# Tanh back to PSUM, factors and blocks on ScalarE, a scan laid out by place, 1.6 pieces of scan for a piece of projection

## The chip, the cores and the metric

One NeuronCore of a Trainium2 chip. The metric is the device time of one launch in microseconds (us), the median of several runs. All data are float32; where TensorE should work at more than one pass of reduced precision, operands are split into a high and a low part ("fp32r") and three products are added.

## The reference, cut to what matters

One layer of a hybrid backbone on 128 context tokens and 2048 latent tokens, 1024 wide:

```python
h = rmsnorm(x, norm_mix) * (1 + sc1) + sh1
u, z_s5, qkv, z_gdn, beta_raw, a_raw = split(dot(h, w_in))
s5_out  = s5_mixer(u, z_s5, ...)      # complex diagonal recurrence, both directions
gdn_out = gdn_mixer(qkv, z_gdn, ...)  # gated DeltaNet in chunks of 64, both directions
x = x + gt1 * dot(concat(s5_out, gdn_out), w_out)
h = rmsnorm(x, norm_mlp) * (1 + sc2) + sh2
x = x + gt2 * dot(square(relu(dot(h, w_mlp_in))), w_mlp_out)
```

Inside the S5 mixer each of 32 channel groups has 64 complex states per direction, `h[t] = abar * h[t-1] + bbar u[t]`, and the output is the real part of `C h` plus a skip, through gelu and a gate. Inside the DeltaNet mixer q, k and v pass a convolution of three taps and SiLU first; each chunk needs the inverse of a unit lower triangular matrix and a decay matrix `exp(g_i - g_j)`.

## The kernel before, in words

**Stages.** The program runs through four stages. Up to some 320 us: setup, the u projection (`first_pass`), the tables of the recurrence (`s5_setup`, `s5_tables`). From some 320 to 1100 us the projection stage: for each of four groups of 512 tokens (0, 3, 1, 2) `group_h` builds the normed rows and `group_proj` multiplies them with the columns of `w_in`, block by block; group 0 stands alone, with the modulation's weights streamed beside it. Then a short stage with the remaining gate columns (`ZCOLS`) and the sequential DeltaNet steps. From some 1412 us to the end phase C: output projection and MLP.

**Work beside the projection.** Generators give up control at each `yield`. After each piece of projection, `Side.go` adds a rate to an account and runs that many pieces of the side work: `first` (DeltaNet, per group: `gdn_front`, `gdn_back`), `second` (`gdn_p2`), `third` (`gdn_p3`) and `scans` (eight parts `s5_part`, 15 pieces each). The rate of `scans` is 2 in the projection stage (L1734) and 3 in the next (where `second.rate, third.rate, scans.rate` are set). The program is then ordered on each engine by a planner's own timeline, so a rate sets an order of birth, and the planner what comes out of it.

**Eviction, `evac` L479.** A block of a projection (258 or 387 columns in a PSUM bank of the pool `psd`, three banks) goes through five operations: ScalarE takes the middle tap (L491), VectorE adds the two others from the bank (L493, L495), ScalarE takes tanh (L497) into a tile `ec2` of SBUF, VectorE forms (tanh + 1) * y (L499), and a DMA writes the result to DRAM. The bank's last reader is L495.

**Factors.** In `gdn_back` the decay matrix E of a chunk and direction (128 x 4 heads x 128) comes from four exponentials (L696) and is multiplied by a factor per row and head on GpSimd (L697); VectorE uses it at once. In `gdn_load` the loaded keys are multiplied by their decay in the same way (L873). In `gdn_p3`, which joins the inverses of blocks of 32 to a block of 128, the rows `RW` of four blocks come by DMA and GpSimd spreads them over block diagonal tiles TA and R by multiplying them, repeated, with a mask Mh or Mb of zeros and ones (L762, L764).

**The scan, `s5_part` L1254.** One part handles four channel groups, in both directions; a lane holds 8 sequences (2 directions, real and imaginary, 2 groups) of 272 elements in time order, one sequence behind the other, each with 17 super-chunks of 16 places. One element here stands for 8 tokens, whose inner steps are in the tables. First, for places 1 to 15, all super-chunks at once take one step of the recurrence (L1301 two products, L1303 and L1305 sums): every operand is read or written every 16th element. Then 15 steps carry the state from one super-chunk to the next, one after the other (L1323, L1325, L1326, on 16 and 8 elements). Then the entering states, times the powers of abar, are added to all elements (GpSimd product L1335, VectorE sum L1338). TensorE reads the states for the output (L1356), for the backward direction in reverse order.

**What the page calls them.** Tile names are those in the code: E, KVr, R, TA, Hin, S, T (for `T1`), gs (a PSUM bank of the scan), d (a bank of the projection), ec (the eviction's tiles).

Of the kernel before, what the change touches and what calls it, by code (L numbers as in the profile page):

```python
# [478 lines left out]
def evac(k, ct, ps, n, segs, off):  # L479
    nc = k.nc  # L480
    S = k.S
    if ct < 8:
        z = k.pe.tile([128, k.pew], F32, name="ec1")
        nc.scalar.activation(z[:, 0:n], ps[:, off:off + n], AF.Tanh, scale=0.5)
        nc.vector.tensor_scalar(z[:, 0:n], z[:, 0:n], 0.25, 0.25, op0=OP.mult, op1=OP.add)
        for (o, m, tk) in segs:
            nc.sync.dma_start(S['tz'][(ct - 4) * 128:(ct - 3) * 128, tk:tk + m], z[:, o:o + m])
    elif ct < 20:
        q = ct - 8
        t1 = k.pe.tile([128, k.pew], F32, name="ec1")  # L490
# [8 lines left out]
        nc.vector.scalar_tensor_tensor(o_[:, 0:n], th[:, 0:n], 1.0, y2[:, 0:n], op0=OP.add, op1=OP.mult)  # L499
# [51 lines left out]
def gdn_setup(k):  # L551

    nc = k.nc
    k.Mb = k.ga.tile([128, 4], F32, name="Mb")
# [14 lines left out]
    nc.gpsimd.memset(k.Mb, 0.0)  # L569
    nc.gpsimd.memset(k.Mh, 0.0)  # L570
    for b in range(4):
        nc.gpsimd.memset(k.Mb[32 * b:32 * b + 32, b:b + 1], 1.0)
        nc.gpsimd.memset(k.Mh[32 * b:32 * b + 32, b % 2:b % 2 + 1], 1.0)
# [175 lines left out]
def gdn_p3(k, cs):  # L749
# [6 lines left out]
    TA = k.ga.tile([128, 2, 4, 64], F32, name="TA")[:, 0:n]  # L756
    R = [k.ga.tile([128, 2, 4, 128], F32, name=f"R{d}")[:, 0:n] for d in range(2)]
    for j, c in enumerate(cs):
        nc.sync.dma_start(RW[:, j].rearrange("p d w h c->p (d w h) c"), dap(S['rw'], c * 65536, [[32, 128], [4096, 16], [1, 32]]))
        for d in range(2):  # L760
            pairs, a, e = PAIRS[d]
            nc.gpsimd.tensor_tensor(TA[a, j].rearrange("p h (b c)->p h b c", b=2), RW[a, j, d, 1, :, None, :].to_broadcast([64, 4, 2, 32]),  # L762
                                    k.Mh[a, None, :, None].to_broadcast([64, 4, 2, 32]), op=OP.mult)
            nc.gpsimd.tensor_tensor(R[d][:, j].rearrange("p h (b c)->p h b c", b=4), RW[:, j, d, 0, :, None, :].to_broadcast([128, 4, 4, 32]),  # L764
                                    k.Mb[:, None, :, None].to_broadcast([128, 4, 4, 32]), op=OP.mult)
# [279 lines left out]
def s5_setup(k):  # L1045
# [81 lines left out]
    for t_, e in ((k.tab8, 1), (k.tabL, 16)):  # L1127
        nc.vector.tensor_copy(t_[:, 0, 0], P8[:, 0, :, e])
        nc.vector.tensor_copy(t_[:, 0, 1], P8[:, 0, :, e])
        nc.vector.tensor_copy(t_[:, 1, 0], P8[:, 1, :, e])  # L1130
        nc.vector.tensor_scalar(t_[:, 1, 1], P8[:, 1, :, e], -1.0, None, op0=OP.mult)
# [122 lines left out]
def s5_part(k, hb):  # L1254
# [36 lines left out]
    def cols(t):  # L1291

        return t.rearrange("p r (d c)->p d r c", d=2)[:, :, :, c0:c0 + 2]
    TB8 = sb.tile([128, 2, 8], F32, name="tb8", bufs=1)
    TBL = sb.tile([128, 2, 8], F32, name="tbL", bufs=1)
    for t_, s_ in ((TB8, k.tab8), (TBL, k.tabL)):
        for j in range(2):
            V.tensor_copy(t_[:, j].rearrange("p (d r g)->p d r g", d=2, r=2), cols(s_[:, j]))
    for kk in range(1, 16):
        Tt = sb.tile([128, 2, 136], F32, name="Tt", bufs=1)  # L1300
        V.tensor_tensor(Tt.rearrange("p j (a s)->p j a s", a=8), sview(S, kk, [[0, 2], [272, 8], [16, 17]]), TB8[:, :, :, None].to_broadcast([128, 2, 8, 17]), op=OP.mult)  # L1301
        av = sview(S, 1 + kk, [[16, 136]])
        V.tensor_tensor(av, av, Tt[:, 0], op=OP.add)  # L1303
        sv = sview(S, 1 + kk, [[1088, 2], [544, 2], [16, 34]])
        V.tensor_tensor(sv, sv, Tt[:, 1].rearrange("p (d r a)->p d r a", d=2, r=2)[:, :, ::-1], op=OP.add)  # L1305
        if kk % 4 == 3:
            yield None
    for d in range(2):
        V.tensor_copy(k.NS[:, :, 16 * d + c0:16 * d + c0 + 2], sview(S, row(d, 0, 0) + 272 - 256 * d, [[544, 2], [272, 2]]))

    Hin = sb.tile([128, 2, 2, 2, 17], F32, name="Hin", bufs=1)
    H0 = Hin.rearrange("p d r g s->p (d r g s)")
    V.memset(sview(H0, 16, [[52, 2], [17, 4]]), 0.0)

    def hat(s_):
        return sview(H0, s_, [[69, 2], [17, 4]])

    def hat3(s_):
        return sview(H0, s_, [[69, 2], [34, 2], [17, 2]])
    V.tensor_copy(hat3(0), cols(k.h0))  # L1320
    for sc in range(15):
        Tb = sb.tile([128, 2, 8], F32, name="Tb", bufs=1)
        V.tensor_tensor(Tb.rearrange("p j (d a)->p j d a", d=2), sview(H0, sc, [[0, 2], [69, 2], [17, 4]]),  # L1323
                        TBL.rearrange("p j (d a)->p j d a", d=2), op=OP.mult)
        V.tensor_tensor(hat(sc + 1), sview(S, 1 + sc * 16 + 15, [[1088 + 16, 2], [272, 4]]), Tb[:, 0].rearrange("p (d a)->p d a", d=2), op=OP.add)  # L1325
        V.tensor_tensor(hat3(sc + 1), hat3(sc + 1), Tb[:, 1].rearrange("p (d r g)->p d r g", d=2, r=2)[:, :, ::-1], op=OP.add)  # L1326
    yield None
    for d in range(2):
        cs = slice(16 * d + c0, 16 * d + c0 + 2)
        for ri in range(2):  # L1330
            for j in range(2):
                oi = ri if j == 0 else 1 - ri
                tab = k.P8[:, j, cs, 1:17]
                T1 = sb.tile([128, 2, 17, 16], F32, name="T1", bufs=2)
                nc.gpsimd.tensor_tensor(T1, Hin[:, d, ri, :, :, None].to_broadcast([128, 2, 17, 16]),  # L1335
                                        tab[:, :, None, :].to_broadcast([128, 2, 17, 16]), op=OP.mult)
                sv = sview(S, row(d, oi, 0) + 1, [[1, 544]])
                V.tensor_tensor(sv, sv, T1.rearrange("p g s k->p (g s k)"), op=OP.subtract if ri == 1 and j == 1 else OP.add)  # L1338
        yield None

    for d in range(2):
        lat, ctx = (0, 256) if d == 0 else (16, 0)
        V.tensor_copy(sview(S, row(d, 0, 0) + lat, [[544, 2], [272, 2]]), k.h0[:, :, 16 * d + c0:16 * d + c0 + 2])
        V.memset(sview(S, row(d, 0, 0) + ctx, [[272, 4]]), 0.0)
# [527 lines left out]
```

## Time and profile before

| | |
|---|---|
| time, median of 3 runs | 3263.98 us (3262.58 to 3274.36) |
| profiled execution | 3273.32 us, its span 3271.5 us |
| mean granted TensorE clock | 0.949 of full speed |
| PE busy | 2968.4 us, 91% |
| VectorE (DVE) busy | 2012.6 us, 62% |
| GpSimd (POOL) busy | 1387.3 us, 42% |
| ScalarE (ACT) busy | 1106.4 us, 34% |
| DMA | 604.36 MB, 185 GB/s in the mean |

How to read it: busy time is the time in which an engine executes; PE stands for TensorE's matmuls. A page cuts the span in 40 slices of 82 us and gives each engine's busy share in tenths, so a stage is seen by its slices. A row of a view by lines gives busy time in us, mean ns of one, and the idle time before it with what ended it; rows of waits give us in total, times, and the longest. The rows on which the argument rests stand in a section of their own below.

### The profile page before, as it was taken

What the parts mean: (1) busy time and instruction counts of PE and PEld (TensorE: products, weight loads), DVE (VectorE), ACT (ScalarE), POOL (GpSimd) and SP (SyncE); (2) the same over time, 40 slices, a digit from 0 to 9 for tenths busy, and PEclk for the clock granted to TensorE, in tenths of its full rate; (3) what the DMA queues carried; (4) which work ended last, traced back from release to release, by engine and by line L of the source; (5) the groups of instructions that cost most, each with busy time, mean ns of one, the idle gap of its engine ahead of it and who ended that gap; (6) DMA issues with size and microseconds to landing.
All of it is one profiled execution on the core that took longest, in us unless ns stands there. A gap on an engine that the chain in (4) does not pass through costs nothing. (4 is left out here: it accounts for less than half of the span.)

```text
span 3271.5 us, 48561 instructions
## 1 busy us (share of the span) xinstructions
PE 2968.4 (91%) x17658; PEld 2520.8 (77%) x17658; DVE 2012.6 (62%) x3901; ACT 1106.4 (34%) x2325; POOL 1387.3 (42%) x1027
## 2 busy tenths in 40 slices
PE   5785879998898899988999999999999999999998
PEld 3673668787777777977887778898888887888886
DVE  5975587896877676346544367543458643684445
ACT  3442224543443221234333233322243322433332
POOL 3562232423345233146443454333444544554542
PEclk8887899999987999989999999999999999999999
DMA  9899967867667987989433455322434534553332
GB/s 261 198 182 258 332 207 229 262 216 240 206 204 237 285 279 255 361 289 328 138 103 107 147 166 166 100 78 78 139 123 150 150 94 126 164 170 98 99 95 71
DMA packets 573504, 604.36 MB, mean 185 GB/s; under 512 B 163020, under 2 KB 422208, under 8 KB 573264
## 3 DMA queue, kind: packets, MB, share of 16 engines
q1 hardware_dynamic: 573264, 601.25, 59.9%
q8 instruction: 139, 2.28, 0.3%
q14 instruction: 101, 0.83, 0.1%
HBM read 458.99 MB, written 142.14 MB: 184 GB/s over the span
## 5 line engine op out<-in xcount | busy, mean ns | idle before, releaser
L1400 POOL TENSOR_TENSOR wol<-woraw,woh 128x512 fp32r<-128x512 f32 x320 | 427.7, 1348 | 644.4 <-ACT woh L1399 629.1
L1550 DVE TENSOR_TENSOR acc<-acc,gA 128x512 f32<-128x512 f32 x510 | 340.9, 682 | 196.1 <-PE gA L1545 195.9
L1399 ACT ACTIVATE woh<-woraw 128x512 fp32r<-128x512 f32 x320 | 193.0, 626 | 777.3 <-PE gA L1545 467.9
L1545 PE MATMUL gA<-woh,ffH 128*128 128x512 f32 x1088 | 425.2, 391 | 5.7 <-ACT r L1527 3.2
L1545 PE MATMUL gA<-woh,ffL 128*128 128x512 f32 x1088 | 424.7, 390 | 1.9 <-DVE ffL L1531 1.9
L1545 PE MATMUL gA<-wol,ffH 128*128 128x512 f32 x1088 | 424.1, 390 | 0.0
L1400 POOL TENSOR_TENSOR wil<-wiraw,wih 128x1024 fp32r<-128x1024 f32 x128 | 327.2, 2557 | 114.3 <-PE gA L1523 81.9
L1530 DVE TENSOR_TENSOR r<-r 128x512 f32<-128x512 f32 (+1 forms) x160 | 167.1, 1051 | 306.5 <-ACT ffH L1529 306.2
L1523 PE MATMUL gA<-htH,wih 128*128 128x512 f32 (+1 forms) x1280 | 277.7, 362 | 4.5 <-DVE acc L1550 3.2
L1523 PE MATMUL gA<-htL,wih 128*128 128x512 f32 (+1 forms) x1280 | 272.8, 358 | 0.0
L1523 PE MATMUL gA<-htH,wil 128*128 128x512 f32 (+1 forms) x1280 | 271.8, 357 | 0.0
L471 PE MATMUL d<-hH,wh 128*128 128x258 f32 (+3 forms) x1152 | 212.7, 326 | 52.4 <-DMA wh<-s_wc 15.3
L1523 PEld LDWEIGHTS gA<-htH,wih 128*128 128x128 f32 x1280 | 223.3, 190 | 37.5 <-DVE acc L1550 4.5
L1523 PEld LDWEIGHTS gA<-htL,wih 128*128 128x128 f32 x1280 | 221.7, 188 | 30.8
L1523 PEld LDWEIGHTS gA<-htH,wil 128*128 128x128 f32 x1280 | 220.5, 188 | 29.9
L1545 PEld LDWEIGHTS gA<-woh,ffH 128*128 128x128 f32 x1088 | 204.8, 188 | 49.8 <-ACT r L1527 4.2
L1545 PEld LDWEIGHTS gA<-woh,ffL 128*128 128x128 f32 x1088 | 204.8, 188 | 44.1 <-DVE ffL L1531 2.3
L1545 PEld LDWEIGHTS gA<-wol,ffH 128*128 128x128 f32 x1088 | 204.8, 188 | 42.8
L471 PEld LDWEIGHTS d<-hH,wh 128*128 128x128 f32 x1152 | 178.7, 205 | 75.3 <-issue 31.9
L471 PE MATMUL d<-hL,wh 128*128 128x258 f32 (+3 forms) x1152 | 211.9, 319 | 3.6 <-DMA hL<-s_hL 3.5
L471 PE MATMUL d<-hH,wl 128*128 128x258 f32 (+3 forms) x1152 | 210.7, 321 | 3.3 <-DMA wl<-s_wc 3.3
L471 PEld LDWEIGHTS d<-hH,wl 128*128 128x128 f32 x1152 | 179.5, 202 | 17.3 <-issue 10.7
(387 smaller groups left out, 5407.4 us busy)
## 6 DMA issues: line engine op xcount, KB each, us to landing
wiraw<-in_w_mlp_in SPq DMA_DIRECT2D x128, 512.0 KB
woraw<-in_w_mlp_out SPq DMA_DIRECT2D x256, 256.0 KB
wl<-s_wc SPq DMA_DIRECT2D x68, 512.0 KB
wh<-s_wc SPq DMA_DIRECT2D x68, 512.0 KB
wada<-in_w_ada SPq DMA_DIRECT2D x48, 512.0 KB
KVr<-s_kv SPq DMA_DIRECT2D x34, 512.0 KB
Qr<-s_qkv SPq DMA_DIRECT2D x32, 512.0 KB
woraw<-in_w_out SPq DMA_DIRECT2D x64, 256.0 KB
```

The costliest lines, as they stand in the source:

```text
L471: nc.tensor.matmul(ps[:, 0:w], W_[:, kk, :], X_[kk][:, f:f + w], start=(n == 0), stop=(n == 23))
L1399: nc.scalar.activation(h[:, i:i + n], w, AF.Copy)
L1400: sub.tensor_tensor(l[:, i:i + n], w, h[:, i:i + n].bitcast(F32), op=OP.subtract)
L1523: nc.tensor.matmul(ps[b][:, 0:w], W[:, kk, :], X[:, kk, b * w:b * w + w], start=(m == 0), stop=(m == 23))
L1530: nc.vector.tensor_tensor(r[:, 0:w], r[:, 0:w], r[:, 0:w], op=OP.mult)
L1545: nc.tensor.matmul(ps, X[:, s], W[:, hf], start=(m == 0), stop=(m == 3 * FB - 1))
L1550: nc.vector.tensor_tensor(accs[i][:, c], accs[i][:, c], ps, op=OP.add)
```

## The change

Five edits are made together.

- `evac`: tanh (L497) writes to the block's own PSUM bank, and L499 reads it there.
- `gdn_back` and `gdn_load`: the GpSimd products L697 and L873 become four ScalarE operations each (copy with a scale per row), one for each head.
- `gdn_p3`: TA and R are persistent tiles, zeroed once in `gdn_setup`; ScalarE copies the blocks that are not zero, 12 copies for each call in place of two GpSimd products for each of the two directions and each chunk of the call.
- `s5_part`, `s5_setup`, `lane_tables`: the states are laid out by place: element 17 * place + super-chunk, with the row stride 289, so that one place of all super-chunks lies side by side. The carry over the super-chunks goes in four doubling steps over all of them, with a table `tabs` of five powers (1, 16, 32, 64, 128) in place of 15 single steps. ScalarE writes the input (L1287) and TensorE reads the states (L1356) with a stride of 17.
- the rate of the scans in the projection stage goes from 2 to 1.6.

```diff
@@ evac
-        th = k.pe.tile([128, k.pew], F32, name="ec2")
-        nc.scalar.activation(th[:, 0:n], y2[:, 0:n], AF.Tanh)
+        th = ps[:, 0:n]
+        nc.scalar.activation(th, y2[:, 0:n], AF.Tanh)
...
@@ gdn_setup
+    k.TA = k.ga.tile([128, 2, 4, 64], F32, name="TA")
+    k.R = [k.ga.tile([128, 2, 4, 128], F32, name=f"R{d}") for d in range(2)]
+    for t in (k.TA, *k.R):
+        nc.gpsimd.memset(t, 0.0)
...
@@ gdn_back
-        nc.gpsimd.tensor_tensor(E, E, bc4(bb[:, d]), op=OP.mult)
+        for h in range(4):
+            nc.scalar.activation(E[:, h], E[:, h], AF.Copy, scale=bb[:, d, h:h + 1])
@@ gdn_p3
-        for d in range(2):
-            pairs, a, e = PAIRS[d]
-            nc.gpsimd.tensor_tensor(TA[a, j]..., RW[a, j, d, 1, :, None, :]..., k.Mh..., op=OP.mult)
-            nc.gpsimd.tensor_tensor(R[d][:, j]..., RW[:, j, d, 0, :, None, :]..., k.Mb..., op=OP.mult)
...
+    for d in range(2):
+        pairs, a, e = PAIRS[d]
+        for blk in range(4):
+            nc.scalar.activation(R[d][sl(blk), :, :, sl(blk)], RW[sl(blk), :, d, 0], AF.Copy)
+            if sl(blk).start in (a.start, a.start + 32):
+                nc.scalar.activation(TA[sl(blk), :, :, sl(blk % 2)], RW[sl(blk), :, d, 1], AF.Copy)
@@ gdn_load
-    nc.gpsimd.tensor_tensor(KV[:, 0], KV[:, 0], bc4(k.kd[:, c, d]), op=OP.mult)
+    for h in range(4):
+        nc.scalar.activation(KV[:, 0, h], KV[:, 0, h], AF.Copy, scale=k.kd[:, c, d, h:h + 1])
@@ s5_setup
-    for t_, e in ((k.tab8, 1), (k.tabL, 16)):
...
+    Ls = p.tile([128, 2, 4, 32], F32, name="Ls")
+    nc.vector.tensor_copy(Ls[:, :, 0], P8[:, :, :, 16])
+    for i in range(3):
+        cmul(nc.vector, Ls[:, 0, i + 1], Ls[:, 1, i + 1], Ls[:, 0, i], Ls[:, 1, i], Ls[:, 0, i], Ls[:, 1, i], tmp[:, :, 0])
+    for e in range(5):
...
@@ s5_part
-    S = su.tile([128, 1 + 8 * 272], F32, name="S")
+    E = su.tile([128, 8 * 289], F32, name="S")
...
-                nc.scalar.activation(o if d == 0 else o[:, ::-1], ps[:, 0:272], AF.Copy)
+                o = sview(E, r + 17, [[1, 17], [17, 16]]) if d == 0 else sview(E, r + 288, [[-1, 17], [-17, 16]])
+                nc.scalar.activation(o, ps[:, 0:272].rearrange("p (s c)->p s c", c=16), AF.Copy)
...
     for kk in range(1, 16):
-        V.tensor_tensor(Tt..., sview(S, kk, [[0, 2], [272, 8], [16, 17]]), TB8..., op=OP.mult)
-        av = sview(S, 1 + kk, [[16, 136]])
+        V.tensor_tensor(Tt..., sview(E, 17 * kk, [[0, 2], [289, 8], [1, 17]]), tab(0, 17), op=OP.mult)
+        av = sview(E, 17 * kk + 17, [[289, 8], [1, 17]])
...
-    for sc in range(15):
...
+    for i in range(4):
+        sh = 1 << i
+        n = 16 - sh
+        Tb = sb.tile([128, 2, 136], F32, name="Tt", bufs=1)[:, :, 0:8 * n].rearrange("p j (a s)->p j a s", a=8)
+        V.tensor_tensor(Tb, sview(Hin, 1, [[0, 2], [18, 8], [1, n]]), tab(1 + i, n), op=OP.mult)
+        hv = sview(Hin, 1 + sh, [[18, 8], [1, n]])
+        V.tensor_tensor(hv, hv, Tb[:, 0], op=OP.add)
+        hv = sview(Hin, 1 + sh, [[72, 2], [18, 4], [1, n]])
+        V.tensor_tensor(hv, hv, Tb[:, 1].rearrange("p (r a) s->p r a s", r=2)[:, ::-1], op=OP.add)
...
-                h = S[la, r:r + 272]
-                nc.tensor.matmul(y, CA[la, ri, d, g, :], h if d == 0 else h[:, ::-1],
+                h = sview(E[la], r, [[1, 17], [17, 16]]) if d == 0 else sview(E[la], r + 271, [[-1, 17], [-17, 16]])
+                nc.tensor.matmul(y, CA[la, ri, d, g, :], h,
@@ program
-            scans = Side(2, [s5_part(k, hb) for hb in range(8)])
+            scans = Side(1.6, [s5_part(k, hb) for hb in range(8)])
```

## Rows read from the trace of the kernel before

**Rows 1.** Slices of the page: busy tenths in 40 slices of the span.
```profile
PE   5785879998898899988999999999999999999998
DVE  5975587896877676346544367543458643684445
```
**Rows 2.** Stretches: from:to, length, PE, PEld, DVE, ACT, POOL, clock, DMA share, GB/s.
```profile
1600.00:3271.50 1671.50, 1627.69 (x7744) 1380.93 (x7743) 905.81 (x1168) 533.09 (x884) 767.71 (x472) 0.99 0.39 121
...
500.00:550.00 50.00, 48.12 (x363) 41.86 (x362) 36.02 (x94) 23.19 (x71) 8.18 (x7) 1.00 0.72 234
1050.00:1100.00 50.00, 47.92 (x402) 36.58 (x402) 26.05 (x51) 20.98 (x60) 19.53 (x20) 0.87 0.90 269
...
550.00:600.00 50.00, 44.76 (x322) 41.52 (x321) 49.83 (x165) 24.49 (x79) 17.72 (x14) 0.93 0.69 224
1100.00:1150.00 50.00, 39.19 (x315) 37.05 (x314) 41.71 (x124) 9.50 (x21) 9.56 (x9) 0.86 0.93 301
...
320.00:480.00 160.00, 126.19 (x673) 93.50 (x674) 116.22 (x277) 35.75 (x68) 45.19 (x28) 0.89 0.82 272
100.00:200.00 100.00, 81.34 (x675) 74.86 (x675) 93.16 (x193) 46.66 (x92) 70.73 (x49) 0.90 0.88 207
```
**Rows 3.** Waits of PE, 480 to 1150: us in total, times, longest us.
```profile
PE gT L691 <- DVE qn L650: 9.5, 6, 2.4
...
PE gT L649 <- ACT kv L639: 3.8, 4, 1.8
...
PE d L471 <- DVE Hin L1326: 0.3, 1, 0.3
```
**Rows 4.** First group: ACT's waits, and DVE and PE in time (start, us).
```profile
ACT ec L491 <- DVE ec L499: 34.3, 6, 9.0
...
369.39 0.62 DVE L495 SCALAR_TENSOR_TENSOR ec<-d,cw,ec 128x385 f32<-128x385 f32 x1
...
388.24 0.89 DVE L499 SCALAR_TENSOR_TENSOR ec<-ec,ec 128x385 f32<-128x385 f32 x2
...
417.95 2.06 PE L471 MATMUL d<-hH,wh 128*128 128x258 f32 x8 [7.52 <-DVE ec L495]
```
**Rows 5.** Scan by line (ns min/median/max) and by form (busy us, mean ns).
```profile
L1301 DVE TENSOR_TENSOR Tt<-S,tb x120: 586/621/1628, 308.3 to 1237.7; 128x272 f32<-128x272 f32 x120
L1305 DVE TENSOR_TENSOR S<-S,Tt x120: 367/395/2484, 310.1 to 1238.7; 128x136 f32<-128x136 f32 x120
L1325 DVE TENSOR_TENSOR Hin<-S,Tb x120: 153/168/2359, 333.8 to 1254.6; 128x8 f32<-128x8 f32 x120
...
L1323 DVE TENSOR_TENSOR Tb<-Hin,tbL 128x16 f32<-128x16 f32 x120 | 32.9, 274 | 1.3
L1325 DVE TENSOR_TENSOR Hin<-S,Tb 128x8 f32<-128x8 f32 x120 | 27.8, 232 | 1.4
...
L736 DVE TENSOR_TENSOR UB<-W,U 128x256 f32<-128x256 f32 x5 | 2.1, 421 | 0.0
```
**Rows 6.** GpSimd lines by form: busy us, mean ns, idle before and what ended it.
```profile
L697 POOL TENSOR_TENSOR E<-E,bb 128x512 f32<-128x512 f32 x34 | 40.8, 1199 | 119.9 <-ACT E L696 39.6 <-issue 20.0 <-DVE UB L736 9.4
L873 POOL TENSOR_TENSOR KVr<-KVr,kd 128x512 f32<-128x512 f32 x34 | 38.7, 1138 | 72.3 <-DMA KVr<-s_kv 65.2 <-PE gs L1356 7.0
...
L762 POOL TENSOR_TENSOR TA<-RW,Mh 64x256 f32<-64x256 f32 x34 | 24.2, 711 | 36.5 <-DMA RW<-s_rw 31.9 <-ACT UC L706 3.1
```
**Rows 7.** ScalarE lines of the sizes that the change adds, by form.
```profile
L973 ACT ACTIVATE o<-o,ors 128x128 f32<-128x128 f32 x68 | 21.9, 391 | 26.3 <-POOL ors L80 26.3
L703 ACT ACTIVATE UC<-Us 64x256 f32<-64x256 f32 x34 | 14.1, 415 | 54.5 <-DVE Us L700 51.6 <-PE g L801 2.4
```
**Rows 8.** The scan's output matmul, and ScalarE reads strided and contiguous, by form.
```profile
L1356 PE MATMUL gs<-S,CA 64*128 64x272 f32 x256 | 58.6, 445 | 19.0 <-DVE S L1344 19.0
...
L1271 ACT ACTIVATE WT<-T 128x512 f32<-128x512 f32 x8 | 8.6, 1070 | 6.5 <-PE gs L1351 6.5
L1216 ACT ACTIVATE WI<-gs 128x512 f32<-128x512 f32 x16 | 8.9, 584 | 7.2 <-DMA s_stab<-WI 3.7 <-PE gs L1215 3.4
```

More of the change, by code (lines that the diff above doesn't have):

```diff
@@ L495, in evac @@
         nc.vector.scalar_tensor_tensor(y2[:, 0:n], ps[:, 2:2 + n], k.cw[:, 2, q:q + 1], y[:, 0:n], op0=OP.mult, op1=OP.add)
[L496 to L497 removed]
+        th = ps[:, 0:n]
+        nc.scalar.activation(th, y2[:, 0:n], AF.Tanh)
         o_ = k.pe.tile([128, k.pew], F32, name="ec3")
[L499 removed]
+        nc.vector.scalar_tensor_tensor(o_[:, 0:n], th, 1.0, y2[:, 0:n], op0=OP.add, op1=OP.mult)
         for (o, m, tk) in segs:
@@ L553, in gdn_setup @@
     nc = k.nc
-    k.Mb = k.ga.tile([128, 4], F32, name="Mb")
-    k.Mh = k.ga.tile([128, 2], F32, name="Mh")
+    k.TA = k.ga.tile([128, 2, 4, 64], F32, name="TA")
+    k.R = [k.ga.tile([128, 2, 4, 128], F32, name=f"R{d}") for d in range(2)]
+    for t in (k.TA, *k.R):
+        nc.gpsimd.memset(t, 0.0)
     k.mr_neg = k.ga.tile([128, 2, 128], FR, name="mneg")
@@ L568, in gdn_setup @@
     nc.vector.tensor_copy(k.rsel, sel)
[L569 to L573, printed above, removed]
 def gdn_scalars(k, b):
@@ L755, in gdn_p3 @@
     RW = k.gx.tile([128, 2, 2, 2, 4, 32], F32, name="RW")[:, 0:n]
-    TA = k.ga.tile([128, 2, 4, 64], F32, name="TA")[:, 0:n]
-    R = [k.ga.tile([128, 2, 4, 128], F32, name=f"R{d}")[:, 0:n] for d in range(2)]
+    TA = k.TA[:, 0:n]
+    R = [r[:, 0:n] for r in k.R]
     for j, c in enumerate(cs):
         nc.sync.dma_start(RW[:, j].rearrange("p d w h c->p (d w h) c"), dap(S['rw'], c * 65536, [[32, 128], [4096, 16], [1, 32]]))
-        for d in range(2):
-            pairs, a, e = PAIRS[d]
[L762 to L765, printed above, removed]
     def sl(blk):
         return slice(32 * blk, 32 * blk + 32)
+    for d in range(2):
[4 more added lines that the diff above has]
+                nc.scalar.activation(TA[sl(blk), :, :, sl(blk % 2)], RW[sl(blk), :, d, 1], AF.Copy)
     pg = k.psI.tile([128, 512], F32, name="g3")
@@ L981 @@
 PI = float(np.pi)
-SCRATCH_S = {'ys': [512, 8, 272], 'stab': [4, 128, 5120], 'sp': [128, 1408]}
+SCRATCH_S = {'ys': [512, 8, 272], 'stab': [4, 128, 5120], 'sp': [128, 1792]}
 def exp_acc(k, out, x, tag):
@@ L1032, in lane_tables @@
     k.P8 = SP[:, 0:1088].rearrange("p (r c e)->p r c e", r=2, c=32)
-    k.tab8 = SP[:, 1088:1216].rearrange("p (j r c)->p j r c", j=2, r=2)
-    k.tabL = SP[:, 1216:1344].rearrange("p (j r c)->p j r c", j=2, r=2)
-    k.h0 = SP[:, 1344:1408].rearrange("p (r c)->p r c", r=2)
+    k.tabs = SP[:, 1088:1728].rearrange("p (e b j q)->p e b j q", e=5, b=8, j=2)
+    k.h0 = SP[:, 1728:1792].rearrange("p (r c)->p r c", r=2)
 def s5_load(k):
-    SP = k.sp.tile([128, 1408], F32, name="SPl")
+    SP = k.sp.tile([128, 1792], F32, name="SPl")
     k.nc.sync.dma_start(SP, k.S['sp'])
@@ L1065, in s5_setup @@
     lre, lim, ldt = lanes[:, 0], lanes[:, 1], lanes[:, 2]
-    SP = p.tile([128, 1408], F32, name="SP")
+    SP = p.tile([128, 1792], F32, name="SP")
     lane_tables(k, SP)
@@ L1125, in s5_setup, with to @@
     nc.vector.tensor_scalar(k.nPi, Pw[:, 1], -1.0, None, op0=OP.mult)
-    for t_, e in ((k.tab8, 1), (k.tabL, 16)):
[L1128 to L1131, printed above, removed]
+    Ls = p.tile([128, 2, 4, 32], F32, name="Ls")
[3 more added lines that the diff above has]
+    for e in range(5):
+        re_, im_ = [(P8[:, r, :, 1] if e == 0 else Ls[:, r, e - 1]).rearrange("p (d b g)->p b d g", d=2, b=8) for r in range(2)]
+        def to(j, r):
+            return k.tabs[:, e, :, j].rearrange("p b (r d g)->p b r d g", r=2, d=2)[:, :, r]
+        nc.vector.tensor_copy(to(0, 0), re_)
+        nc.vector.tensor_copy(to(0, 1), re_)
+        nc.vector.tensor_copy(to(1, 0), im_)
+        nc.vector.tensor_scalar(to(1, 1), im_, -1.0, None, op0=OP.mult)
     nc.sync.dma_start(k.S['sp'], SP)
@@ L1267, in s5_part @@
     nc.sync.dma_start(CA.rearrange("p r d g c->p (r d) (g c)"), dap(k.S['stab'], base + 2048 + hf * 256, [[5120, 128], [512, 4], [1, 256]]))
-    WE = sb.tile([128, 2, 17, 16], F32, name="T1", bufs=2).rearrange("p a b c->p (a b c)")[:, 0:512].rearrange("p (g e c)->p g e c", g=4, e=8)
+    WE = sb.tile([128, 2, 16, 17], F32, name="T1", bufs=2).rearrange("p a b c->p (a b c)")[:, 0:512].rearrange("p (g e c)->p g e c", g=4, e=8)
     nc.sync.dma_start(WE.rearrange("p g e c->p (g e c)"), dap(k.S['stab'], base + 4096 + hf * 512, [[5120, 128], [1, 512]]))
@@ L1271, in s5_part @@
     nc.scalar.activation(WT, WE.rearrange("p g e c->p g c e"), AF.Copy)
-    S = su.tile([128, 1 + 8 * 272], F32, name="S")
+    E = su.tile([128, 8 * 289], F32, name="S")
     def row(d, ri, g):
-        return (d * 4 + ri * 2 + g) * 272
+        return (ri * 4 + d * 2 + g) * 289
     for g in range(2):
@@ L1291, in cols, with tab @@
     def cols(t):
[L1293 to L1298, printed above, removed]
+        return t.rearrange("p r (d c)->p r d c", d=2)[:, :, :, c0:c0 + 2]
+    def tab(e, n):
+        return k.tabs[:, e, hb, :, :, None].to_broadcast([128, 2, 8, n])
@@ L1306, in s5_part @@
+        av = sview(E, 17 * kk + 17, [[289, 8], [1, 17]])
+        V.tensor_tensor(av, av, Tt[:, 0].rearrange("p (a s)->p a s", a=8), op=OP.add)
+        sv = sview(E, 17 * kk + 17, [[1156, 2], [289, 4], [1, 17]])
+        V.tensor_tensor(sv, sv, Tt[:, 1].rearrange("p (r a s)->p r a s", r=2, a=4)[:, ::-1], op=OP.add)
         if kk % 4 == 3:
             yield None
+    Hin = sb.tile([128, 144], F32, name="Hin", bufs=1)
+    V.memset(Hin, 0.0)
+    V.tensor_copy(sview(Hin, 1, [[72, 2], [36, 2], [18, 2]]), cols(k.h0))
@@ L1308, in s5_part @@
     for d in range(2):
[L1309 to L1320, printed above, removed]
@@ L1321, in s5_part @@
-    for sc in range(15):
[L1322 to L1326, printed above, removed]
+        V.tensor_copy(sview(Hin, 36 * d + 2, [[72, 2], [18, 2], [1, 15]]), sview(E, row(d, 0, 0) + 272 + d, [[1156, 2], [289, 2], [1, 15]]))
@@ new lines, in s5_part @@
+        V.tensor_copy(k.NS[:, :, 16 * d + c0:16 * d + c0 + 2], sview(E, row(d, 0, 0) + 272 + 16 - 16 * d, [[1156, 2], [289, 2]]))
+    for i in range(4):
[7 more added lines that the diff above has]
+        V.tensor_tensor(hv, hv, Tb[:, 1].rearrange("p (r a) s->p r a s", r=2)[:, ::-1], op=OP.add)
@@ L1327, in s5_part, with enter @@
     yield None
+    def enter(d, ri):
+        return (ri * 4 + d * 2) * 18 + 1 - d
     for d in range(2):
@@ L1332, in s5_part @@
                 oi = ri if j == 0 else 1 - ri
[L1333 to L1338, printed above, removed]
+                t = k.P8[:, j, cs, 1:17]
+                T1 = sb.tile([128, 2, 16, 17], F32, name="T1", bufs=2)
+                nc.gpsimd.tensor_tensor(T1, sview(Hin, enter(d, ri), [[18, 2], [0, 16], [1, 17]]),
+                                        t[:, :, :, None].to_broadcast([128, 2, 16, 17]), op=OP.mult)
+                sv = sview(E, row(d, oi, 0) + 17, [[289, 2], [1, 272]])
+                V.tensor_tensor(sv, sv, T1.rearrange("p g k s->p g (k s)"), op=OP.subtract if ri == 1 and j == 1 else OP.add)
+        V.tensor_copy(sview(E, row(d, 0, 0), [[1156, 2], [289, 2], [1, 17]]), sview(Hin, enter(d, 0), [[72, 2], [18, 2], [1, 17]]))
         yield None
[L1341 to L1344, printed above, removed]
     Y = su.tile([128, 4, 272], F32, name="Y")
```

6 lines of the change are left out of this document (1 added, 5 removed).

## The prediction, made before the result was known

> **What bounds the kernel now.** I read the slices of the page first, then the stretches, then the lines inside them. The page's slices show PE at nine tenths or more from half of the span on, and DVE at eight or nine tenths only in the first third [rows 1]. From 1600 us to the end PE is busy 1627.69 of 1671.50 us at a granted clock of 0.99 [rows 2]; no line there is touched, so that half is left at its time. The change works between about 320 us (first projection block) and 1600 us, and in the table setup before it.
>
> There the stretches differ. I compare them by "rate": the busy share of PE times its granted clock. In the stretches where DVE is lightly loaded (50 us each from 500, 600, 750, 900 and 1050; DVE 154.4 of 250 us, 62%) the rate is 0.96, 0.85, 0.92, 0.84 and 0.83, mean 0.88. In those where DVE is full (550 to 600, 650 to 750, 800 to 900, 950 to 1050, 1100 to 1150; 358.3 of 400 us, 90%) it is 0.83, 0.85, 0.77, 0.68 and 0.67, by length 0.76. The first group's stretch, 320 to 480, has 0.79 x 0.89 = 0.70 [rows 2]. So in the projection stage PE is the bound, and a full DVE takes 12 points of its rate away. The waits of PE from 480 to 1150 say the same from the other side: twelve rows name DVE, 44 us in 28 waits, from 9.5 down to 0.3 us [rows 3]. In 320 to 480 the evictions are the gate: ACT's first step L491 waits 34.3 us for DVE L499, six times, and PE waits for a bank that L495 frees [rows 4].
>
> **The change, part by part.** *Scan by place* (DVE). The three operations of a step read or write every 16th element now: 272 elements in a median of 621 ns, 136 in 395 ns. The nearest unit-stride row is L736's 421 ns for 256 elements; a line from L1325's 168 ns for 8 to it has 1.02 ns an element, which gives 437 and 298 ns [rows 5]. Saved: 120 x 0.184 + 240 x 0.097 = 45 us. The serial chain over 16 super-chunks is three lines, L1323 to L1325 at 32.9 to 27.8 us, 91 us in 360 small operations [rows 5]; four doubling steps make 12 operations a part, 32 of 240 down to 128 elements (about 0.37 us by the same line, with a little for POOL) and 64 of 120 down to 64 (about 0.27 us), together 29 us: 62 us saved. The copies that go and those that come (initial state, prefixes) are some 0.2 us each and cancel.
>
> *Factors and blocks on ScalarE.* POOL loses four lines of 34 instructions each, from 40.8 us (L697) to 24.2 (L762), 140.8 us together [rows 6]. DVE has a part in this: an operation of 8 elements, L1325, takes 168 ns in the median, up to 2359 ns, and 232 ns in the mean [rows 5]; something other than its size holds it. [...] From the rows alone: 64 ns over its median, in six such lines of 120, are 46 us that the scan's operations lose; with 140.8 us less on POOL I take a little under half, 20 us, an estimate. DVE is thus relieved of 45 + 62 + 20 = 127 us, some 110 of them before 1150 us. In 320 to 480 and the ten other stretches DVE is at 629 of 810 us [rows 2]; 519 are left, 64%, which is the load of the light stretches if it is spread evenly. **1.6 instead of 2** does that: a part yields 15 times, eight parts 120 times; the stage steps the scans 64 times, so 2 ends them at its 60th step and 1.6 leaves 18 pieces to the next stage, where the rate is 3. Gain: 400 us x (1 - 0.76/0.88) = 53 us, and 160 us x (1 - 0.70/0.88) = 33 us in the first stretch, of which I take 25, since weights for the modulation are streamed there as well (DMA share 0.82). Bounds: nothing (PE waits for others) and 53 + 33 = 86 us, with 10 more if the light stretches gain too.
>
> What ScalarE takes on: 2 x 136 operations of 128x128 with a factor, 391 ns by L973, 106 us, and 9 calls of `gdn_p3` x 12 copies of 32 x 256, 415 ns by L703, 45 us [rows 7]: 151 us over 1100 us. ACT is at 19 to 49% there [rows 2], so it goes to some 60% at most. The four factor operations (1.6 us) replace one of 1.2 us on POOL. Two waits move: POOL now waits 31.9 us for RW and 65.2 us for KVr to land [rows 6]; on ACT the first eviction step L491, Exp, the copies of G and w and, later, the weight splits are queued behind them. Cost between less than nothing (POOL's queue was the later one) and 97 us (ACT is never later and all behind it is needed); the largest of PE's rows that name ACT in 480 to 1150 is 3.8 us [rows 3], so I take 5.
>
> *PE reads the scan strided.* L1356's moving operand was contiguous (272 columns); now each column lies 17 elements from the last. It has 256 records, two to a matmul, 58.6 us busy: 229 ns a record, 0.84 ns a column and pass [rows 8]. The trace has no strided moving operand. Below: no change (a slower one can't be excluded, a faster one can: the reads are the same in number). Above: ScalarE needs 1070 ns for 512 elements read 16 apart against 584 ns for contiguous ones, +0.95 ns an element [rows 8]; on PE 272 x 0.95 x 256 = 66 us. DVE pays (621 - 437)/272 = 0.68 ns, which gives 47 us. I take DVE's, with 0.88 of it on the path: 41 us. [...] The strided write of ScalarE (L1287, 64 operations) may cost as much an element, 17 us on an engine that has room.
>
> *Tanh in PSUM.* L497 and L499 keep their sizes; what changes is that the bank of a block is freed by L499, no longer by L495. In 320 to 480 L495 of a block of 385 columns ends at 370.0, its L499 starts at 388.24 [rows 4]; L491 waits for L499 six times there, once for each pair of blocks. Price between nothing (the lighter DVE brings L499 forward; the order is planned anew) and 6 x 7.52 = 45 us, the wait for a bank that PE shows at 417.95 [rows 4]. I take nothing, because L491 of the next pair waits for this L499 already.
>
> *Setup.* 31 small DVE operations more for the tables (18 in three products, 13 copies), 0.27 us by L1323, 0.42 by L736 [rows 5]: 8 to 13 us on a DVE that is 93% busy from 100 to 200 us [rows 2], where DMA is at 0.88. I take 5; below it is nothing, above 13 us. The memsets on POOL replace ten small ones.
>
> **Sum.** -53 - 25 + 41 + 5 + 5 = -27 us. The profiled execution took 3273.32 us, its span 3271.5; so 3246. The median of the runs shown is 3263.98, 9 us less; on that basis 3237 us.
>
> **Rivals.** *PE's strided read is free.* For it: PE takes 0.84 ns a column in this form, twice DVE's speed, and may have the room; against it: both other engines pay. Then -27 - 41 = -68: 3196 us. *DVE was not the gate.* The full stretches also hold other PE work, and the 44 us of DVE waits in 480 to 1150 [rows 3] are all there is, half of it recovered: -22 - 25 + 41 + 10 = 4: 3268 us, no change. Against it: the five light stretches have the higher rates, with one heavy stretch (0.85) as the exception. *The bank is held until L499* (slower): the mechanism of the paragraph on Tanh. With three banks, PE can run two blocks (24 x 258 and 24 x 385 columns, some 7 us) past a late L499; it decides as soon as L499 lags L495 by more than that, and in the pair shown it lags by 18 us. For it: 34.3 us of waits for L499 [rows 4]. Against it: in the later blocks DVE is to be freed. No gain in the first stretch, 45 us lost, half of the 53 kept: -27 + 45 + 41 + 10 = 69: 3333 us; with the free read 3292.
>
> **How the numbers follow.** The forecast has 0.43, with a range of its own of 3205 to 3262; free read 0.27; no change 0.13; bank held 0.17. About 0.5%, 16 us, is what a measurement of this kernel can tell from no change: faster is below 3248, slower above 3280. Forecast: 0.32 faster, 0.10 same, 0.01 slower; free read: 0.27 faster; no change: 0.03, 0.08, 0.02; bank held: 0.02, 0.02, 0.13. Together 0.64, 0.20, 0.16. The range 3160 to 3300 takes the free read whole with some 35 us for more DVE relief than counted, and of the bank case the mild end.
>
> **What would show it.** L1301, L1303 and L1305 near 440, 295 and 295 ns and the three chain lines gone; L1325's kind of outlier rarer; DVE's share in 320 to 1150 down to about two thirds, spread evenly, and PE's rate in the same stretches near 0.88. L1356's busy time per record says at once whether the strided read costs: 229 ns or some 410. PE's waits for L491, L495 and L499 in the first group show whether banks are held. The prediction is wrong if ACT's waits for RW and KVr stand ahead of PE, if PE's rate stays at 0.76 with DVE at two thirds, or if the part after 1600 us changes its length.

## The result and the profile after

The changed kernel took 3292.32 us in the median (3289.91 to 3295.19, 4 runs) against 3267.71 us of the kernel before (3262.58 to 3274.36, 4 runs): 1.0061 of it by the record, 95% interval 1.0037 to 1.0084; the two medians alone give 1.0075, 25 us. It is slower by 0.6 to 0.8%, where 27 us less were forecast. The profiled execution took 3289.91 us, its span 3288.1 us, 16.6 us more than before.

Where the time went is read at two marks of the program. First, where the last softplus operation of the setup starts (L453) and where the first matmul of the output projection starts (L1437 before, L1441 after); columns: ns min/median/max, first and last start in us. Of the kernel before, then of the changed one:

```profile
L453 DVE TENSOR_SCALAR sp_h<-sp_h x28: 181/183/1308, 155.5 to 282.8; 128x32 f32<-128x32 f32 x21, 128x40 f32<-128x40 f32 x7
...
L1437 PE MATMUL gA<-woh,htH x272: 387/389/793, 1428.1 to 2788.0; 128*128 128x512 f32 x136
```
```profile
L453 DVE TENSOR_SCALAR sp_h<-sp_h x28: 167/182/1440, 161.1 to 291.6; 128x32 f32<-128x32 f32 x21, 128x40 f32<-128x40 f32 x7
...
L1441 PE MATMUL gA<-woh,htH x272: 388/389/796, 1450.0 to 2804.4; 128*128 128x512 f32 x136
```

The setup ends 8.8 us later, the stages in between take 1158 instead of 1145 us, and what follows takes 5 us less. So the stages from 283 to 1428 us are compared as wholes (columns as in [rows 2]: length, busy PE, PEld, DVE, ACT, POOL, clock, DMA share, GB/s), before, and after:

```profile
283.00:1428.00 1145.00, 990.11 (x7616) 842.79 (x7611) 798.32 (x2007) 390.18 (x1042) 377.46 (x356) 0.91 0.79 258
```
```profile
292.00:1450.00 1158.00, 1040.14 (x7612) 860.61 (x7612) 674.66 (x1711) 505.66 (x1373) 253.30 (x233) 0.88 0.79 255
```

VectorE is relieved by 124 us, from 70 to 58% of the stage, and PE does stand idle less: 118 instead of 155 us. But PE is busy 50 us longer with as many instructions, and its mean clock is 0.88 instead of 0.91. What was won as idle time came back as slower matmuls. The lines say which ones and that the removed work is gone as forecast (of the changed kernel, by form, as [rows 5 to 8]):

```profile
L1360 PE MATMUL gs<-S,CA 64*128 64x272 f32 x256 | 101.0, 656 | 4.7 <-DVE S L1346 4.7
...
L1307 DVE TENSOR_TENSOR Tt<-S,SPl 128x272 f32<-128x272 f32 x120 | 60.6, 505 | 34.8 <-ACT S L1295 32.8
L1309 DVE TENSOR_TENSOR S<-S,Tt 128x136 f32<-128x136 f32 x120 | 39.3, 327 | 2.2
L1311 DVE TENSOR_TENSOR S<-S,Tt 128x136 f32<-128x136 f32 x120 | 37.6, 313 | 2.1
L1326 DVE TENSOR_TENSOR Tt<-Hin,SPl 128x240 f32<-128x240 f32 x8 | 3.2, 403 | 0.0
...
L695 ACT ACTIVATE E<-E,bb 128x128 f32<-128x128 f32 x136 | 46.0, 410 | 0.1
L872 ACT ACTIVATE KVr<-KVr,kd 128x128 f32<-128x128 f32 x136 | 43.4, 392 | 16.6 <-DMA KVr<-s_kv 16.5
```

The scan's output matmul has 101.0 us against the 58.6 of [rows 8]. The page's slices, which answer to [rows 1], show nothing of all this but a lighter DVE in the first half:

```profile
PE   5676799998988899988999999999999999999998
DVE  5985655774867662336545367544358643584445
```

### The profile page after: what moved, and what is told of

Read it like the earlier page. It is cut to its first block, busy times and chain, and to the rows that moved or that the text cites. A ratio compares the mean times of both kernels' runs of the same rounds, so it can differ in the third digit from the quotient of the medians.

```text
span 3288.1 us, 48333 instructions
## 1 busy us (share of the span) xinstructions
PE 3014.3 (92%) x17658; PEld 2534.7 (77%) x17658; DVE 1901.1 (58%) x3636; ACT 1238.9 (38%) x2705; POOL 1246.6 (38%) x884
## 5 line engine op out<-in xcount | busy, mean ns | idle before, releaser
L471 PE MATMUL d<-hH,wh 128*128 128x258 f32 (+3 forms) x1152 | 219.4, 331 | 41.7 <-DVE ec L499 18.9
L471 PEld LDWEIGHTS d<-hH,wh 128*128 128x128 f32 x1152 | 181.5, 206 | 73.3 <-issue 48.9
L471 PE MATMUL d<-hL,wh 128*128 128x258 f32 (+3 forms) x1152 | 215.5, 323 | 15.9 <-DMA hL<-s_hL 15.8
L471 PE MATMUL d<-hH,wl 128*128 128x258 f32 (+3 forms) x1152 | 209.7, 320 | 0.0
L471 PEld LDWEIGHTS d<-hL,wh 128*128 128x128 f32 x1152 | 179.6, 203 | 27.8 <-DMA hL<-s_hL 14.9
```

The source lines that it names most:

```text
L471: nc.tensor.matmul(ps[:, 0:w], W_[:, kk, :], X_[kk][:, f:f + w], start=(n == 0), stop=(n == 23))
```

## The experiments

Ratios are the record's, against the kernel before on the same chip in the same runs; those of the medians alone differ from them by up to 0.0024. On the chips of the experiments it takes 3290 to 3291 us, on that of the result 3268. "Same order" means that each engine has the same instructions in the same sequence; where that isn't said, the planner made a new one.

**The strided read, taken away: e1_contig, and e10_contig_again with the same kernel.**

```diff
-                h = sview(E[la], r, [[1, 17], [17, 16]]) if d == 0 else sview(E[la], r + 271, [[-1, 17], [-17, 16]])
-                nc.tensor.matmul(y, CA[la, ri, d, g, :], h,
+                h = E[la, r:r + 272]
+                nc.tensor.matmul(y.rearrange("p (s c)->p c s", c=16), CA[la, ri, d, g, :], h if d == 0 else h[:, ::-1],
```

> The changed kernel, but the matmul that reads the scan's states takes its 272 columns contiguous, in the order of places, and writes them into the PSUM bank 16 elements apart, so that the bank holds the same values. Theory 1 (the strided moving operand is what ate the gain: its busy time went from 58.6 to 101.0 us): busy time back to about 60 us and the time some 35 to 42 us lower, 3250 to 3257 us. Rival (PE had idle time to cover it, and the loss is in the low clock and the waits at the changes of group): busy time falls just the same, but the time stays within 10 us of the changed kernel's 3292. Third: a strided write into PSUM costs PE what the strided read did; then the busy time stays near 100 us.

> e1_contig once more, as the neighbour of the others on the same chip: 0.989 to 0.996 of the kernel before, as the first time (0.9926).

Measured: 0.9926 (0.9901 to 0.9951) and 0.9913 (0.9899 to 0.9927). It is the same order as the changed kernel's on all five engines. The matmul line and the stage of e10_contig_again:

```profile
L1360 PE MATMUL gs<-S,CA 64*128 64x272 f32 x256 | 64.3, 478 | 5.2 <-DVE S L1346 5.2
...
294.00:1406.00 1112.00, 983.96 (x7607) 840.12 (x7608) 671.52 (x1711) 503.63 (x1372) 251.61 (x231) 0.90 0.82 264
```

Theory 1 holds: the strided write into PSUM costs 64.3 - 58.6 = 6 us, the strided read 37 us more than that.

**The same pair again: e17_after_again and e18_strided_r17** (the changed kernel as it is, and with 1.7 for 1.6, the strided twin of e12_contig_r17 below).

> The changed kernel once more, beside the kernel before on one of the chips of the other experiments. If the strided matmul's price at this order is the 1.35% that two comparisons on different chips give: 1.004 to 1.008 of the kernel before. If chips differ in it: outside of that.

> The changed kernel with 1.7 in place of 1.6: the strided twin of e12_contig_r17 (0.9882), with the same instructions in the same order on every engine. Theory 1 (the strided moving operand costs its 37 to 42 us of PE's time whatever the order): 0.999 to 1.003. Rival (part of the 1.35% was the way in which that one order took it): 0.990 to 0.997.

Measured: 1.0039 (1.0020 to 1.0059) and 0.9988 (0.9977 to 1.0000). Each ratio is against the kernel before on its own chip. At rate 1.6 the strided read costs 1.0039 - 0.9913 = 1.26% (41 us), at 1.7 it costs 0.9988 - 0.9882 = 1.06% (35 us). Both expectations are met but for 0.0001 of the first and 0.0002 of the second. A third such pair of the same order, at rate 2, stands among the runs below: 1.0186 (e3_rate2) - 1.0079 (e16_contig_r20) = 1.07%, 35 us. It is the read that costs, not one order.

**VectorE's time at a fixed order: e9_slowdve.**

```diff
-        Tt = sb.tile([128, 2, 136], F32, name="Tt", bufs=1)
+        Tt = sb.tile([128, 2, 136], F32, name="Tt", bufs=1).rearrange("p j e->p (j e)").rearrange("p (s j a)->p j a s", j=2, a=8)
...
```

> e1_contig with the same instructions in the same order on every engine; only the small tile Tt between the three operations of a scan step lies transposed, so that they write and read it 16 elements apart. The price in VectorE time should be near that of the old layout: 621 and 395 ns against 505 and 320, some 30 to 45 us in all. Theory 1 (VectorE isn't what PE waits for in this order): at most 0.3% slower than e1_contig, up to 10 us. Rival (the prediction's: 127 us of VectorE were to give 78 us, so 40 us are worth 25 us): 0.6 to 0.9% slower, 20 to 30 us.

Measured: 0.9982 (0.9972 to 0.9993), 0.69% or 23 us slower than its twin e10_contig_again. Of e9_slowdve:

```profile
L1307 DVE TENSOR_TENSOR Tt<-S,SPl 128x272 f32<-128x272 f32 x120 | 80.0, 667 | 34.3 <-ACT S L1295 32.4
L1309 DVE TENSOR_TENSOR S<-S,Tt 128x136 f32<-128x136 f32 x120 | 53.2, 443 | 2.3
...
292.00:1429.00 1137.00, 992.11 (x7612) 846.42 (x7613) 711.72 (x1712) 503.54 (x1373) 253.56 (x232) 0.90 0.81 259
```

VectorE has 40 us more in the stage (711.72 - 671.52), and the time rises by 23: 0.57 us for each. My theory fell here, and the prediction's price for VectorE (78 us for 127, 0.61) came near, for time that is added at this order. What time taken away is worth at a fixed order, no run shows.

**One part undone: e2_tanh, e3_rate2, e4_pool.** The changed kernel with tanh in SBUF (L497 as before), with `Side(2, ...)`, and with the factors, masks and blocks on GpSimd as before. All three keep the strided read, and the ranges in us are meant for the result's chip.

> The changed kernel with tanh back in its tile of SBUF; all else as changed. Theory 1 (strided read): nothing to see, 3284 to 3300 us. [...]

> The changed kernel with 2 pieces of scan for each piece of projection. Theory 1 (strided read): the work is the same, only its order differs, 3282 to 3302 us. Rival (with 1.6 too little scan work lies at the changes of group, at 620 and 760 us, where PE sits idle and its clock then falls to 0.5): the two dips fill up and the time falls to 3262 to 3275 us.

> The changed kernel with the factors and the blocks back on GpSimd (masks as before); the tanh, the scan and the rate as changed. If the move to ScalarE is what costs (PE waits 8.3 us for E and 7.5 us for RW's followers there, and the exchange of 1.2 us for 1.6 us in a chain): 3275 to 3285 us. [...] If VectorE is not the bound: within 8 us of 3292.

Measured: 1.0111 (1.0081 to 1.0142), 1.0186 (1.0154 to 1.0218) and 1.0101 (1.0075 to 1.0127), each slower than the changed kernel's 1.0039 to 1.0061. No rival that blames one of these edits finds support. On the result's chip the ratios would be 3304, 3328 and 3301 us: all three lie above their ranges, the third by 1 us, and VectorE has 1931.3 us in it against the changed kernel's 1901.1 (711.4 against 674.7 in the stage). How much each edit is worth in time can't be read off, since each has a new order, and those alone move the time by as much:

**The rate alone, in the kernel before: e5_rateonly (1.6), e13_before_r18, e14_before_r22.** One number is changed.

> The kernel before with one number changed: 1.6 instead of 2 pieces of scan for each piece of projection. Theory 1 (2 pieces crowd the projection stage whatever the scan costs VectorE; in the changed kernel going back to 2 cost 1.2%): 0.985 to 0.993 of the kernel before. Rival (the rate fits the cheaper scan, and with the old, longer scan 1.6 leaves too much for the stage behind, where VectorE was 84% busy from 1100 to 1150 us): 0.997 to 1.010.

> The kernel before with 1.8 in place of 2 pieces of scan; the work is the same, the order is planned anew. Theory 1 (a rate of 2 happens to give the kernel before a good order, and any other order costs it some tenths of a per cent): 1.003 to 1.012 of the kernel before. Rival (there is a smooth trend in the rate, 1.6 having cost 0.89%): 1.002 to 1.005. Third (orders scatter to both sides): below 0.998 here or at 2.2.

> The kernel before with 2.2 in place of 2 pieces of scan. Theory 1: 1.003 to 1.012. Rival (smooth, more pieces are better for the old scan): 0.993 to 0.999.

Measured: 1.0089 (1.0063 to 1.0115), 1.0051 (1.0027 to 1.0075), 1.0085 (1.0064 to 1.0107). The stage of e5_rateonly:

```profile
291.00:1465.00 1174.00, 1005.97 (x7611) 853.61 (x7611) 801.53 (x2010) 389.11 (x1041) 372.81 (x355) 0.90 0.78 250
```

The work is the same to 3 us on VectorE and 5 on GpSimd, and the stage is 29 us longer than in the profile of before, 13 of them with PE idle (168 instead of 155); that profile is of the result's chip, where the kernel before takes 22 us less, so a part of this may be the chip. The ratios are free of that: the kernel before at its rate of 2 is the best of its neighbours on both sides, by 0.5 to 0.9%. The expectation that 1.6 would help fell.

**The rate with the contiguous read: e8_contig_r13, e11_contig_r15, e12_contig_r17, e15_contig_r18, e16_contig_r20.**

> e1_contig with 1.3 in place of 1.6 pieces of scan. Theory 1 (the fewer pieces stand in the projection stage, the better, until the next stage ends by them: the last scan's matmul ended 180 us before the output projection at 1.6): 0.985 to 0.992 of the kernel before. Rival (1.6 is where both stages balance, or the scans now end too late): 0.993 to 1.005.

> e1_contig with 1.5 in place of 1.6 pieces of scan: the work is the same, 1062 of 3638 VectorE instructions stand elsewhere in the order. Theory 1 (what the planner makes of a rate moves the time by about 1% without a trend): anywhere from 0.990 to 1.010 of the kernel before, not between its neighbours' 0.9926 (1.6) and 1.0004 (1.3). Rival (a smooth optimum near 1.6): between these two, 0.993 to 0.998.

> e1_contig with 1.7 in place of 1.6 pieces of scan. Theory 1 (scatter of the order): anywhere from 0.990 to 1.010 of the kernel before. Rival (a smooth optimum near 1.6, with 2 some 1.2% worse): 0.993 to 0.999.

> e1_contig with 1.8 pieces of scan. Theory 1 (scatter of orders of about 1%): anywhere from 0.986 to 1.006 of the kernel before, not on a line from 1.7's 0.9882 to 2's. Rival (smooth, with the best near 1.7): 0.987 to 0.993.

> e1_contig with 2 pieces of scan, the rate of the kernel before. The changed kernel at rate 2 had 1.0186; without the 1.3 to 1.4% of the strided matmul that is 1.004 to 1.007 here. If the strided matmul cost more at that order than at 1.6: below 1.002.

| rate | 1.3 | 1.5 | 1.6 | 1.7 | 1.8 | 2 |
|---|---|---|---|---|---|---|
| contiguous read | 1.0004 | 0.9915 | 0.9913 | 0.9882 | 1.0024 | 1.0079 |
| kernel before | | | 1.0089 | | 1.0051 | 1 |
| PE idle in the stage, us, contiguous read | 144 | 126 | 128 | 121 | 150 | 159 |

Each has an interval of about 0.002 to each side. From 1.7 to 1.8 the time jumps by 1.4%, more than the strided read costs, while 1.5 to 1.7 lie close. It is neither a line nor free scatter. The times go with the idle time of PE between the setup's end and the output projection (the stage as above); its busy time there is 977 to 997 us in all six. At rate 2 the ratio is 0.0009 above the range expected. At 1.7 the version with the contiguous read is the fastest of all, 0.9882 (0.9862 to 0.9902) of the kernel before.

**Only the scan, and all but the scan: e6_scanonly, e7_noscan.** The kernel before with the new layout and the contiguous read at rate 2; and the changed kernel with the old scan at 1.6.

> The kernel before with the scan laid out by place alone, its output matmul reading contiguous columns (as in e1_contig); rate 2, tanh in SBUF, factors and blocks on GpSimd as before. VectorE has some 110 us less to do. Theory 1 (VectorE was not what PE waited for, the prediction's sum over rates is wrong): 0.995 to 1.005 of the kernel before. Rival (VectorE's relief is worth what the prediction said, some 53 to 78 us, and it is the other edits that take it back): 0.975 to 0.985.

> The changed kernel with the old scan: tanh in PSUM, factors and blocks on ScalarE, rate 1.6. If the edits add up (changed kernel 1.0061, of which the strided matmul is some 1.3%), what the new layout without its strided matmul brings is read off against e1_contig's 0.9926: theory 1 (VectorE's relief is worth little) expects 0.990 to 0.997 here, the rival (the layout brings the 53 to 78 us, the others take them back) 1.005 to 1.015.

Measured: 1.0074 (1.0051 to 1.0097) and 1.0062 (1.0041 to 1.0082). Both ranges that I had given for the first are missed: a kernel with less work on VectorE and no strided read was slower than before. The second lies in its rival's range. Both differences are as large as what the rate alone did. Beside kernels of the same rate the two disagree: at 1.6 the kernel before has 1.0089, with the other three edits 1.0062, with the scan too 0.9913; at 2 it has 1, with the scan alone 1.0074, with all edits 1.0079. The same scan goes with 1.5% less time at one rate and with 0.7% more at the other, so its worth can't be read off from either.

## Why the prediction was wrong, by its steps

**Scan on VectorE: right.** 45 us were to be saved in three lines by the layout; the three have 137.5 instead of 206.2 us, 69 us less. The medians came to 441 and 299 ns (437 and 298 forecast), and the rest of it goes with the lighter GpSimd, for which 20 us were taken over six lines: with GpSimd's work back, e4_pool has 30 us more on VectorE. That GpSimd is what holds VectorE's operations up was the author's estimate: [rows 5] show the spread of L1325, not its cause. The chain's 91 us became 30 (29 forecast). VectorE's total fell by 111.5 us, about the 127 less the 11 that the setup added.

**Factors and blocks: right in their sizes.** GpSimd lost 140.7 us (140.8), ScalarE took on 132.5 (151). PE's waits that name ScalarE stayed small, 11.8 us from 480 to 1170 us where the kernel before had 10.1 from 480 to 1150. The longest waits of PE in that stretch of the changed kernel are these:

```profile
PE d L471 <- DMA hL<-s_hL: 15.3, 6, 6.5
PE gT L639 <- ACT E L693: 8.3, 2, 6.7
PE g L773 <- DMA RW<-s_rw: 7.5, 4, 5.5
PE gT L688 <- DVE qn L647: 5.6, 2, 4.1
```

The means of the scan's lines fell towards their medians (L1309 327 against 299 ns, before 563 against 401); with GpSimd's work back, in e4_pool, the two sums have means of 340 and 418 ns at medians of 300, and in e6_scanonly, which has that work on GpSimd too, of 375 and 430. These runs have other orders as well, and by what means one engine would hold the other, none of them shows.

**Strided read: right, 41 us forecast.** The line grew by 42.4 us, and undoing it at the same order gave 41, 35 and 35 us. The price per element was borrowed from VectorE's rows, so that it came this near was in part luck. The rival by which PE reads strided for nothing is out: a record of the line has 656 ns in the mean, against 445 before.

**Setup: 5 forecast, 9 measured** in the result's two profiles, of a range that went to 13. On another chip it is less: there the last softplus operation starts at 291.3 and 290.1 us with the old tables (e5_rateonly, e7_noscan) and at 295.5 and 295.0 with the new ones (e6_scanonly, e8_contig_r13).

**Tanh: the bank is held, but it isn't the loss.** In the first group, 320 to 480 us, PE's longest wait for VectorE is this before; then the changed kernel's for PE and for ScalarE (us, times, longest), beside 34.3 us of L491 for L499 in [rows 4]:

```profile
PE d L471 <- DVE ec L495: 15.0, 4, 7.5
```
```profile
PE d L471 <- DVE ec L499: 18.2, 3, 8.1
...
ACT ec L491 <- DVE ec L499: 25.2, 2, 15.4
```

PE now waits for L499, three times, in place of L495. Yet the 24 blocks of the first group (first matmul of L471 to that of the next group) take 168 instead of 174 us, and e2_tanh without that hold is slower, though in a new order. In that stretch of the kernel before, 240 records of L471 with 258 columns are busy for 44.0 us and 247 with 388 for 55.7, so two blocks of 24 are 10 us, where the rival had some 7 and named no row. The rival of 3333 us is out. Its variant with a free read gave 3292 us, the number that was measured; the read was not free, so that is chance.

**What failed is the gain of 53 + 25 us.** It took PE's rate in the stretches where VectorE is light as the rate that the full ones reach once VectorE is relieved. VectorE was relieved, and the rate of the stage stayed: 0.86 x 0.91 = 0.79 before, 0.90 x 0.88 = 0.79 after, the sign of error that the prediction had named. What came instead is 37 us less idle time of PE in the stage (155 to 118), about half of the 78. The waits have the same size: those of PE that name VectorE fell from the 44 us of [rows 3] to 16 in 480 to 1170, and from 31 to 20 in 320 to 480, while new ones came up, for rows from DRAM (hL, 15.3 us against 3.5) and for the blocks RW (7.5 against 0.7). And so have the ratios: all edits without the strided read brought 0.87% (29 us) at rate 1.6, with 4 to 9 us of setup paid. The rival "DVE was not the gate", with half of those 44 us, was nearest for the later stretches.

Why it was half is open between two readings. One is a tacit term: that the order stays. I had treated the rate as a means to spread the load, and the planner's order as given. It is not: orders of the same work differ by 0.5 to 0.9% (before) and by 2% (contiguous read), and the kernel before stood at the best of those tried. At e9_slowdve's price of 0.57 the 124 us of relief would have brought some 70, an estimate that takes time added and time taken away as equal; the rest would then have been lost to the order. The other reading is that VectorE was the gate for less than the rates said. No run held the order of before with the lighter scan, so neither is shown. The gain itself depends on the rate at which it is read: with the contiguous read it is 1.8% at 1.6, 0.3% at 1.8 (not clear of the intervals), and a loss of 0.8% at 2; the means of all rates tried, six and four, are 0.9970 and 1.0056, 28 us apart.

The traces show where the orders differ. The 24 blocks of the first group take 173 to 177 us at the four rates of the kernel before and 158 to 163 at the six with the contiguous read: 11 to 20 us less at any order, where 25 were forecast for 320 to 480 us. From there to the output projection it is 932 us before (957 to 967 at the other three rates, on other chips) and 901 to 948 with the contiguous read. So it is the 53 us of the later groups above all that came out otherwise, and what makes PE wait longer there in one order than in another stays open.

The sum then reads: -29 without the strided read, +41 for it, 12 us: with e17's 1.0039 that is 13 us, in the result's comparison 20 by the ratio and 25 by the medians. The forecast of -27 had the same +41, and -68 in place of -29.

The signs named in the prediction came as follows: the scan's lines, the chain and L1360 as said; VectorE at 58% of the stage, but not spread evenly (45.25 of 50 us from 550 to 600 us, 22.27 of 50 just before); and PE's rate in the stage at 0.79, not 0.88. The rate mixes two things: idle time fell with VectorE's load, and the clock did not rise with it (0.91 before, 0.88 after). By idle time alone the gain would have been sought in 155 us, 34 of them in 320 to 480 [rows 2].

## What to carry to other kernels

When a planner orders the instructions, each edit also draws a new order; change one number that moves no work and time that first, and take its spread as the least error of any forecast by sums. Price a resource at a fixed order, by making the same instructions slower or faster through their strides alone: this told the price of added VectorE time (0.57 us for each us) and TensorE's strided read (35 to 41 us) apart from the order, where undoing edits one by one told little. Compare versions at several rates, not at one: the same scan looked like a gain at 1.6 and like a loss at 2. And lay out data for the engine that bounds the stage: here the stride that VectorE lost was given to TensorE, and a strided write into PSUM was the cheap place for it (6 us instead of 42).

## What the runs showed of the hardware

With the moving operand read 17 elements apart, a record of L1360 (272 columns, two records to a matmul) has 656 ns in the mean, against 445 to 478 with it contiguous. With the output written 16 elements apart in PSUM the line's 256 records take 63.6 us in e1_contig, 64.3 in e10_contig_again and 64.2 in e12_contig_r17, against 58.6 in the kernel before. The granted clock goes with the strided read: at the same order the stage has a mean clock of 0.88 strided and 0.90 contiguous, and over the whole kernel the 13 strided runs at rate 1.6 have 0.935 to 0.939, the 9 contiguous ones 0.944 to 0.948. At rate 1.7 the strided twin shows the same; e18_strided_r17, then e12_contig_r17:

```profile
294.00:1441.00 1147.00, 1040.95 (x7609) 859.14 (x7610) 685.50 (x1711) 504.48 (x1373) 254.91 (x233) 0.89 0.80 257
```
```profile
294.00:1392.00 1098.00, 977.10 (x7612) 833.10 (x7612) 683.89 (x1714) 503.80 (x1374) 257.22 (x233) 0.92 0.83 269
```

PE is busy 64 us longer though the strided line grew by only 104.1 - 64.2 = 40 us; the other 24 us lie in the other instructions, at a lower clock. (These two profiled executions lie 49 us apart, the medians of their kernels 37.) The clock also falls where a new group's rows are late, in the changed kernel from 760 us (5 us a row):

```profile
755.00:760.00 5.00, 2.94 (x18) 1.73 (x14) 0.00 (x0) 0.69 (x2) 1.11 (x2) 1.00 0.63 206
760.00:765.00 5.00, 0.55 (x2) 0.55 (x3) 1.90 (x5) 0.78 (x2) 0.00 (x0) 0.59 0.50 107
765.00:770.00 5.00, 3.56 (x62) 3.13 (x61) 0.00 (x0) 2.02 (x6) 0.00 (x0) 0.50 1.13 273
...
780.00:785.00 5.00, 5.00 (x60) 3.19 (x59) 1.67 (x4) 1.30 (x4) 0.00 (x0) 0.50 1.00 303
790.00:795.00 5.00, 5.00 (x39) 3.58 (x35) 2.09 (x5) 3.01 (x7) 0.00 (x0) 1.00 0.97 203
```

PE waits 6.51 us for a tile of rows from DRAM, and its clock falls to 0.50. It stays there from 765 to 785 us, in which PE is busy 18.56 of 20 us, before it is back at 1.00. Eight records of L1360 take 4.03 us there (from 771.73), where six took 1.57 before the gap (from 754.71): 0.50 against 0.26 us each. At that ratio these 18.56 us hold the work of about 10, an estimate, so this gap of 6.5 us cost more than its length.
